# A gated-DeltaNet and latent-attention trunk on one core: the output norm of the first layer moves from POOL to DVE and ACT

## The chip, the core and the metric

The kernel runs on one core of one Trainium2 chip. Its engines work side by side, each through a queue of its own, in order: PE (TensorE, the matmuls, with the weight loads shown as PEld), DVE (VectorE), ACT (ScalarE), POOL (GpSimd) and SP (SyncE, which issues most of the DMAs). The metric is the device time of one execution in microseconds (us), median of three runs.

## The reference

Two layers over 1040 tokens (16 learned ones and 1024 of the sequence), model width 1024, float32. The first layer is a gated DeltaNet with 8 query/key heads and 16 value heads of width 128, the second latent attention with 16 heads. What the change touches is the end of the first layer's mixer: per value head the result `o` is normalised by its root mean square and then multiplied by the gate `z`.

```python
def gdn_mixer(h, w_in, conv_w, a_log, dt_bias, out_norm, w_out):
    proj = h @ w_in
    ...
    o = gated_delta_rule_chunked(q, k, v, beta, g)
    o = rmsnorm(o, out_norm) * jax.nn.silu(z.astype(jnp.float32).reshape(B, L, GDN_V_HEADS, GDN_DV))
    return o.reshape(B, L, GDN_V_W).astype(h.dtype) @ w_out
```

## The kernel before, in words

The first layer fills about the first 1,070 us, the second the rest. Tokens are cut into 9 chunks (16, then eight of 128; `TOK`) and these into three column groups of 400, 384 and 256 (`NCH`). Matrices are split into a high and a low float32r part, and each product is three matmuls (`proj_part`).

The first layer goes through 8 groups `g`, each one query/key head and two value heads. While the recurrence of group `g` runs over its 9 chunks (`rec_chunk`: `ksp`, `r`, `xps`, `x`, `sps`, `S`, `oq`, `o`, one waiting for the other across PE, DVE and ACT), PE is filled with projections of the next groups (`proj_gen`, tiles `pt`). Their weights come by DMA (`raw`), ACT makes the high part (`whi`, L391), POOL the low part (`wlo`, L392), four buffers of each. Beside that DVE builds, for group `g+1`, the inverses of 32-wide triangular blocks (`fill_m`): a chain in which each step needs the one before, alternating products `pr` (L585, L601, L610) with sums (L587 and L613 into `tu`, L603 into `bm`). It starts with L581 and ends with the last L613; ACT copies its pieces (`bm`, L591, L616, L619).

When the last chunk of a column group has its result, `gate(g, ci, ...)` runs: 8 groups times 3 column groups makes 24 calls. POOL makes the mean square with its floor (L813, L814, tile `ov`) and an inverse square root by a start value and three Newton steps of four instructions (`newton_rsqrt`, L138 to L143, tiles `oy` and `ot`): 15 small instructions on 128x8, 128x6 or 128x4 elements. `scale()` then multiplies each chunk's `o` by `oy` (L820, POOL, 128x256, in 72 instructions over all), and after a delay `out_` transposes it on PE (L831, `tp`), multiplies by `z` on DVE (L833, `gt_`) and writes it to `g1scr`. `later(n, fn)` puts work off by n ticks of the fill; so `scale` comes 9 ticks after `gate`, `out_` 14 after `scale`. POOL also makes `kd` (L740) for the recurrence, masks `gcb` (L544) and has the same Newton steps for the keys (`k_stats`, tiles `yk`, `tk`).

Nothing in the text fixes the order on an engine: a scheduler orders the instructions by readiness and priority, so a moved instruction also shifts its neighbours. [...]

Of the kernel before, what the change touches and what calls it, by code (L numbers as in the profile page):

```python
# [15 lines left out]
P = 128  # L16
# [29 lines left out]
def build(nc, tc, A, out, dbg=None):  # L46
# [89 lines left out]
    def newton_rsqrt(e, y, v, t):  # L136

        e.tensor_scalar(y.bitcast(I32), v.bitcast(I32), -0.5, float(0x5F3759DF), op0=ALU.mult, op1=ALU.add)  # L138
        for _ in range(3):
            e.tensor_tensor(t, v, y, op=ALU.mult)  # L140
            e.tensor_tensor(t, t, y, op=ALU.mult)
            e.tensor_scalar(t, t, -0.5, 1.5, op0=ALU.mult, op1=ALU.add)
            e.tensor_tensor(y, y, t, op=ALU.mult)  # L143
# [28 lines left out]
    with contextlib.ExitStack() as g_es:  # L172
# [14 lines left out]
        with tp_(name="xp", bufs=1) as xpool:  # L187
            xts = []
            stats = gp.tile([P, 403], F32, name="stats", tag="xpad", bufs=3)
            xbanks = iter([('tp', 4), ('tp', 4), ('tp', 4), ('tp', 4), ('tp', 4), ('tp', 4), ('tp', 4), ('tp', 4), ('tp', 4), ('tp', 4), ('tp', 4), ('tp', 4), ('tp', 4), ('tp', 4), ('tp', 4), ('tp', 4), ('tp', 4), ('tp', 4), ('tp', 4), ('tp', 4), ('tp', 4), ('tp', 4), ('tp', 4), ('tp', 4)])  # L190
            for (n0, n, cs) in NCH:
                for c in cs:
                    t0, tn = TOK[c]
                    tag = next(xtags)
                    if tag == "MT":
                        xw = gp.tile([P, 8, 2, 128], F32, name="xt", tag=tag, bufs=2).rearrange("p a b c -> p (a b c)")
                        xt = xw[:, :D]
                    elif tag == "mt":
                        xt = xw[:, D:]
                    elif tag:  # L200
                        xt = gp.tile([P, L], F32, name="xt", tag=tag, bufs=2)[:, :D]
                    else:
                        xt = xpool.tile([P, D], F32, name="xt", bufs=5)
                    sp.dma_start(xt[:tn], A["meta_tokens"] if c == 0 else A["x"][t0 - 16:t0 - 16 + tn])
                    if c == 0:
                        junk = gp.tile([P, L], F32, name="junk", tag="vT", bufs=1)[:, :D]
                    ss, rs = stats[:, c:c + 1], stats[:, 16 + c:17 + c]
                    act.activation(junk[:tn], xt[:tn], AF.Square, accum_out=ss[:tn])
                    rstd(gp, rs[:tn], ss[:tn], D, dve if c in (1, 3, 6, 8) else pool)
                    dve.tensor_scalar(xt[:tn], xt[:tn], rs[:tn], None, op0=ALU.mult)  # L210
                    xts.append(xt)

            w_in = A["gdn_w_in"][0].rearrange("(k p) c -> p k c", p=P)
            first_w = []
            first_t = [gp.tile([P, 1024], F32, name="wf", tag=f"u{x}", bufs=1).bitcast(F32R) for x in range(2)]
            for kq in range(4):
                raw = wp.tile([P, 2, 128], F32, name="raw", bufs=4)
                sp.dma_start(raw, w_in[:, 2 * kq:2 * kq + 2, QKW:QKW + 128])
                hl = [first_t[x][:, 256 * kq:256 * kq + 256].rearrange("p (k c) -> p k c", k=2) for x in range(2)]
                act.copy(hl[0], raw)  # L220
                pool.tensor_tensor(hl[1], raw, f(hl[0]), op=ALU.subtract)
                first_w.append(hl)
            first_pts = [ps.tile([P, 512], F32, name="pt", tag="proj", bufs=3) for _ in NCH]
            for pi, (n0, n, cs) in enumerate(NCH):
                for d in range(KT):
                    pt = ps.tile([P, 512], F32, name="pt", **dict(zip(("tag", "bufs"), next(xbanks))))
                    for c in cs:
                        t0, tn = TOK[c]
                        xt = xts[c]
                        pe.transpose(pt[:, t0 - n0:t0 - n0 + tn], xt[:tn, d * 128:(d + 1) * 128], ident[:tn, :tn])  # L230
                    act.activation(hsh[d][:, n0:n0 + n], pt[:, :n], AF.Copy, scale=vecs[:, PN0 + d:PN0 + d + 1])
                    dve.scalar_tensor_tensor(hsl[d][:, n0:n0 + n], pt[:, :n], vecs[:, PN0 + d:PN0 + d + 1],
                                             f(hsh[d][:, n0:n0 + n]), op0=ALU.mult, op1=ALU.subtract)
                for k in range(KT):
                    hi, lo = first_w[k // 2]
                    proj_part(first_pts[pi], hi[:, k % 2], lo[:, k % 2], k, n0, n)
# [568 lines left out]
        def gate(g, ci, os_, oss):  # L805

            s = st[g]
            n0, nn, cs = NCH[ci]
            nc_ = len(cs)
            v = gp.tile([P, 4, 2], F32, name="ov", bufs=2)  # L810
            y = gp.tile([P, 4, 2], F32, name="oy", bufs=3)
            t = gp.tile([P, 4, 2], F32, name="ot", bufs=2)
            pool.tensor_scalar(v[:, :nc_], oss[:, :nc_], 1.0 / 128.0, None, op0=ALU.mult)  # L813
            pool.tensor_tensor(v[:, :nc_], v[:, :nc_], s["q2e"][:, cs[0]:cs[0] + nc_].unsqueeze(2).broadcast_to([P, nc_, 2]), op=ALU.add)  # L814
            newton_rsqrt(pool, y[:, :nc_], v[:, :nc_], t[:, :nc_])

            def scale():
                for i, c in enumerate(cs):
                    n = TOK[c][1]
                    pool.tensor_tensor(os_[i][:n], os_[i][:n], y[:n, i].unsqueeze(2).broadcast_to([n, 2, 128]), op=ALU.mult)  # L820
                later(OUT7 if g == 7 else OUTL, lambda: out_(0), False)

            def out_(h):
                if len(s["z"]) < 2:
                    later(3, lambda: out_(h), False)
                    return
                tp = ps.tile([P, 512], F32, name="tp", tag="tr", bufs=1)

                for i, c in enumerate(cs):
                    t0 = TOK[c][0]  # L830
                    pe.transpose(tp[:, t0 - n0:t0 - n0 + 128], os_[i][:, h], ident)  # L831
                gt_ = gp.tile([P, 400], F32, name="gt_", tag="tanh", bufs=3)
                dve.scalar_tensor_tensor(gt_[:, :nn], tp[:, :nn], onh, s["z"][h][ci], op0=ALU.mult, op1=ALU.mult)  # L833
                r0 = (2 * g + h) % 4 * 128
                (pool if g == 7 else sp).dma_start(g1scr[(2 * g + h) // 4][r0:r0 + 128, n0:n0 + nn], gt_[:, :nn])
                s["gated"] = s.get("gated", 0) + 1
                if h == 0:
                    later(3, lambda: out_(1), False)
            later(SC7 if g == 7 else SCL, scale, False)
# [886 lines left out]
```

## Time and profile before

| | us |
|---|---|
| median of the runs (2162.71, 2164.35, 2171.89) | 2164.35 |
| the profiled execution | 2172.86 |
| its span | 2170.8 |
| PE busy in the span | 2044.1 (94%) |
| DVE, ACT, POOL busy | 1353.9, 1102.1, 745.2 |
| the first layer, about | 1,070 of 2,170.8 |

The profiled execution lies 0.4% above the median. Busy time is that of one engine's instructions; what matters is where PE, the fullest engine, stands idle or runs at the lower of its two clock levels, and which engine it then waits for. A row of the timeline gives the start, the time, the engine, the line, the operation and the tiles; x3 behind it merges three alike in sequence, and in brackets stands the idle time before it and who ended it.

### The profile page before, as it was taken

The page shows a single profiled execution, that of the slowest core. Times are in us where ns is not written, and L with a number is a line of the kernel's source. Part 1 is how long each engine was busy: PE and PEld are TensorE (multiplying, and loading weights), DVE is VectorE, ACT ScalarE, POOL GpSimd, SP SyncE. Part 2 cuts the span into 40 slices and gives each one's busy share as a digit, 9 for nine tenths or more (in the row PEclk, how much of TensorE's full clock was granted, in tenths as well). Part 3 has the DMA queues.
Part 4 walks back from the last instruction along what each step waited for, and adds up shares of the span by engine and source line. Part 5 has one row for each costly group of instructions (what it writes and reads, how often), then busy time and mean ns, then how long its engine had stood idle before and what let it go on. Part 6 is the DMA issues. An engine that isn't in the chain of part 4 may idle for free.

```text
span 2170.8 us, 38605 instructions
## 1 busy us (share of the span) xinstructions
PE 2044.1 (94%) x13407; PEld 1823.2 (84%) x13407; DVE 1353.9 (62%) x3135; ACT 1102.1 (51%) x3323; POOL 745.2 (34%) x1718
## 2 busy tenths in 40 slices
PE   7789889999899999999799999999999999999998
PEld 6789778989899998987576898888999999987886
DVE  6485848585758586765345653436787777885422
ACT  5745545656464746454334453435565656664311
POOL 4442636445554544441301472301304032010111
PEclk9999989999999999999999999999999999999999
DMA  3222122222122222124445431221111111124431
GB/s 119 65 52 60 41 68 58 60 59 64 45 72 54 69 57 63 47 66 110 138 109 171 139 98 61 88 97 45 40 50 40 47 37 50 40 81 163 158 100 41
DMA packets 237419, 164.01 MB, mean 76 GB/s; under 512 B 78476, under 2 KB 217304, under 8 KB 237224
## 3 DMA queue, kind: packets, MB, share of 16 engines
q1 hardware_dynamic: 225472, 140.12, 22.9%
q0 software_dynamic: 4128, 13.15, 1.6%
q10 hardware_dynamic: 7624, 8.27, 1.2%
q8 instruction: 106, 1.74, 0.3%
q14 instruction: 89, 0.73, 0.1%
HBM read 121.27 MB, written 40.19 MB: 74 GB/s over the span
## 4 chain that ended last, share of the span: by engine, by line
PE 57%; DVE 6%; DMA 3%; ACT 2%; POOL 2%; issue 2%; SPq 0%; DVEq 0%; ACTq 0%; POOLq 0%
PE b_a L63 27%; PE b_tr L63 8%; PE pt L63 8%; PE b_pv L63 5%; PE b_tr L1510 3%; PE oq L63 1%; DMA raw<-in_gdn_w_out 1%; DVE pr L585 1%; DMA wraw<-in_gdn_w_out 1%; PE b_tr L1408 1%; PE sps L63 1%; PE b_tr L1504 1%; PE xps L63 1%; PE b_tr L1629 1%; DVE vT L429 1%
## 5 line engine op out<-in xcount | busy, mean ns | idle before, releaser
L63 PE MATMUL pt<-hsh,wlo 128*128 128x400 f32 (+2 forms) x1128 | 370.2, 333 | 17.1 <-POOL wlo L392 17.1
L63 PE MATMUL pt<-hsh,whi 128*128 128x400 f32 (+2 forms) x1128 | 374.4, 333 | 7.4 <-DVE zs L664 3.2
L63 PE MATMUL pt<-hsl,whi 128*128 128x400 f32 (+2 forms) x1128 | 367.5, 326 | 0.0
L392 POOL TENSOR_TENSOR wlo<-raw,whi 128x256 fp32r<-128x256 f32 x188 | 155.6, 833 | 269.5 <-ACT whi L391 251.1
L63 PEld LDWEIGHTS pt<-hsh,wlo 128*128 128x128 f32 x1128 | 213.3, 191 | 20.1 <-POOL wlo L392 19.2
L63 PEld LDWEIGHTS pt<-hsh,whi 128*128 128x128 f32 x1128 | 215.3, 191 | 11.3 <-DVE zs L664 3.6
L63 PEld LDWEIGHTS pt<-hsl,whi 128*128 128x128 f32 x1128 | 214.9, 191 | 1.1
L1486 POOL COPY p<-p 128x32 f32<-128x32 f32 x128 | 28.3, 221 | 338.6 <-ACT p L1483 319.3
L1483 ACT ACTIVATE p<-b_a,mx 128x256 f32<-128x256 f32 (+4 forms) x224 | 120.8, 546 | 39.0 <-DVE mx L1475 17.5
L60 DVE TENSOR_TENSOR ptl<-b_tr,pth 128x512 fp32r<-128x512 f32 x192 | 104.6, 549 | 24.2 <-ACT pth L59 21.9
L59 ACT CAST pth<-b_tr 128x512 fp32r<-128x512 f32 x192 | 91.5, 487 | 52.7 <-PE b_tr L1510 51.3
L1468 DVE TENSOR_REDUCE mx<-b_a 128x1 f32<-128x256 f32 (+4 forms) x224 | 110.9, 504 | 10.5 <-PE b_a L63 7.0
L59 ACT CAST gh<-graw 128x512 fp32r<-128x512 f32 (+1 forms) x86 | 51.1, 602 | 126.2 <-PE b_a L63 87.0
L391 ACT CAST whi<-raw 128x256 fp32r<-128x256 f32 x188 | 75.2, 406 | 66.4 <-PE pt L63 27.5
L60 DVE TENSOR_TENSOR gl<-graw,gh 128x512 fp32r<-128x512 f32 x82 | 55.7, 688 | 82.4 <-ACT gh L59 82.2
L429 DVE SCALAR_TENSOR_TENSOR vT<-xpad,wcv,vT 128x256 f32<-128x256 f32 (+2 forms) x144 | 85.3, 635 | 23.0 <-ACT xpad L423 21.7
L1510 PE MATMUL b_tr<-cm,p 128*128 128x128 f32 x576 | 93.7, 274 | 1.4 <-ACT wt L1390 0.7
L63 PE MATMUL b_a<-hsh,gh 128*128 128x512 f32 (+1 forms) x224 | 88.3, 401 | 6.1 <-ACT ojunk L995 4.2
L1309 DVE SCALAR_TENSOR_TENSOR wlo<-raw,vecs,whi 128x128 fp32r<-128x128 f32 x128 | 44.7, 379 | 72.2 <-ACT whi L1308 69.1
L63 PE MATMUL b_a<-hsl,gh 128*128 128x512 f32 (+1 forms) x224 | 87.9, 400 | 0.3
L740 POOL TENSOR_TENSOR kd<-ktok,kds 128x256 f32<-128x256 f32 x72 | 48.0, 666 | 115.2 <-PE sps L63 114.6
L63 PE MATMUL b_a<-ckth,qah 128*128 128x256 f32 (+4 forms) x224 | 81.5, 364 | 3.2 <-ACT p L1483 3.2
(610 smaller groups left out, 6073.8 us busy)
## 6 DMA issues: line engine op xcount, KB each, us to landing
raw<-in_gdn_w_in SPq DMA_DIRECT2D x192, 128.0 KB
graw<-g1scr SPq DMA_DIRECT2D x52, 256.0 KB
raw<-in_mla_w_in SPq DMA_DIRECT2D x64, 128.0 KB
zscr<-z SPq DMA_DIRECT2D x16, 512.0 KB
zh<-zscr SPq DMA_DIRECT2D x32, 256.0 KB
g2scr<-g2t POOLq DMA_DIRECT2D x32, 256.0 KB, 3.4
graw<-g2scr SPq DMA_DIRECT2D x30, 256.0 KB
wraw<-in_mla_w_out SPq DMA_DIRECT2D x13, 512.0 KB
```

Of the source, the lines that this page charges most:

```text
L59: act.copy(hi, src)
L60: dve.tensor_tensor(lo, src, f(hi), op=ALU.subtract)
L63: pe.matmul(out_, l, r, start=start, stop=stop)
L391: act.copy(hi, raw)
L392: pool.tensor_tensor(lo, raw, f(hi), op=ALU.subtract)
L429: dve.scalar_tensor_tensor(o, xp[:, j:j + n], wc(j), o, op0=ALU.mult, op1=ALU.add)
L740: pool.tensor_tensor(kd, s["ktok"][c].unsqueeze(1).broadcast_to([P, 2, 128]), s["kds"][:, c].unsqueeze(2).broadcast_to([P, 2, 128]), op=AL ...
L1309: dve.scalar_tensor_tensor(lo[:, i], raw[:, i], gk, f(hi[:, i]), op0=ALU.mult, op1=ALU.subtract)
L1468: dve.tensor_reduce(mx[:, i:i + 1], o, axis=AX.X, op=ALU.max, negate=(m == 1))
L1483: act.activation(p[:, bd[i]:bd[i + 1]], pts[i][:, :n], AF.Exp, bias=nm, accum_out=rsum[:, i:i + 1])
L1486: pool.tensor_copy(pm[:, 0:32].rearrange("p (r k) -> p r k", r=2), p[:, 0:16].unsqueeze(1).broadcast_to([P, 2, 16]))
L1510: pe.transpose(tp[:kn, i * 128:(i + 1) * 128], ps4[i][:, 32 + kt0:32 + kt0 + kn], ident)
```

## The change

Three things. In `gate`, the 15 small instructions go from POOL to DVE. In `scale`, each POOL multiply of 128x256 becomes two ACT instructions of 128x128, one per head, which copy with a per-partition factor. And the first `pt` of the transposes is taken before the three first projection tiles, so tag `tp` gets the first four PSUM banks and `proj` the next three.

```diff
--- before.py
+++ after.py
@@ -220,10 +220,12 @@
                 act.copy(hl[0], raw)
                 pool.tensor_tensor(hl[1], raw, f(hl[0]), op=ALU.subtract)
                 first_w.append(hl)
-            first_pts = [ps.tile([P, 512], F32, name="pt", tag="proj", bufs=3) for _ in NCH]
+            first_pts = []
             for pi, (n0, n, cs) in enumerate(NCH):
                 for d in range(KT):
                     pt = ps.tile([P, 512], F32, name="pt", **dict(zip(("tag", "bufs"), next(xbanks))))
+                    if not first_pts:
+                        first_pts = [ps.tile([P, 512], F32, name="pt", tag="proj", bufs=3) for _ in NCH]
                     for c in cs:
                         t0, tn = TOK[c]
                         xt = xts[c]
@@ -810,14 +812,15 @@
             v = gp.tile([P, 4, 2], F32, name="ov", bufs=2)
             y = gp.tile([P, 4, 2], F32, name="oy", bufs=3)
             t = gp.tile([P, 4, 2], F32, name="ot", bufs=2)
-            pool.tensor_scalar(v[:, :nc_], oss[:, :nc_], 1.0 / 128.0, None, op0=ALU.mult)
-            pool.tensor_tensor(v[:, :nc_], v[:, :nc_], s["q2e"][:, cs[0]:cs[0] + nc_].unsqueeze(2).broadcast_to([P, nc_, 2]), op=ALU.add)
-            newton_rsqrt(pool, y[:, :nc_], v[:, :nc_], t[:, :nc_])
+            dve.tensor_scalar(v[:, :nc_], oss[:, :nc_], 1.0 / 128.0, None, op0=ALU.mult)
+            dve.tensor_tensor(v[:, :nc_], v[:, :nc_], s["q2e"][:, cs[0]:cs[0] + nc_].unsqueeze(2).broadcast_to([P, nc_, 2]), op=ALU.add)
+            newton_rsqrt(dve, y[:, :nc_], v[:, :nc_], t[:, :nc_])
 
             def scale():
                 for i, c in enumerate(cs):
                     n = TOK[c][1]
-                    pool.tensor_tensor(os_[i][:n], os_[i][:n], y[:n, i].unsqueeze(2).broadcast_to([n, 2, 128]), op=ALU.mult)
+                    for h in range(2):
+                        act.activation(os_[i][:n, h], os_[i][:n, h], AF.Copy, scale=y[:n, i, h:h + 1])
                 later(OUT7 if g == 7 else OUTL, lambda: out_(0), False)
 
             def out_(h):
```

Lines of the changed kernel are 2 or 3 higher from there on: `wlo` L392 becomes L394, `x` L760 becomes L762, the DVE chain L585, L587, L601, L603 becomes L587, L589, L603, L605. The first 1,217 PE instructions stand as before; in the second layer only a handful of neighbours change places.

POOL in the period of group 4, at the end of the first column group's gate. Before:

```order
L140 TENSOR_TENSOR ot<-ov,oy 128x8
L141 TENSOR_TENSOR ot<-ot,oy 128x8
L142 TENSOR_SCALAR ot<-ot 128x8
L143 TENSOR_TENSOR oy<-oy,ot 128x8
L820 TENSOR_TENSOR o<-o,oy 16x256
L820 TENSOR_TENSOR o<-o,oy 128x256 x3
L392 TENSOR_TENSOR wlo<-raw,whi 128x256 x2
L420 MEMSET xpad 128x3
L392 TENSOR_TENSOR wlo<-raw,whi 128x256
L740 TENSOR_TENSOR kd<-ktok_6497,kds 128x256
```

The same place in the changed kernel:

```order
L394 TENSOR_TENSOR wlo<-raw,whi 128x256
L546 TENSOR_TENSOR gcb<-gcb,cm 128x384 x2
L394 TENSOR_TENSOR wlo<-raw,whi 128x256 x2
L742 TENSOR_TENSOR kd<-ktok_6522,kds 128x256
L394 TENSOR_TENSOR wlo<-raw,whi 128x256 x2
L422 MEMSET xpad 128x3
L394 TENSOR_TENSOR wlo<-raw,whi 128x256
L742 TENSOR_TENSOR kd<-ktok_6522,kds 128x256
```

The Newton steps and the multiplies `o<-o,oy` are gone from ahead of the `wlo` rows.

DVE in the same period, inside the inverse chain. Before:

```order
L601 TENSOR_TENSOR pr<-tu,bm 64x256
L603 TENSOR_REDUCE bm<-pr 64x64
L601 TENSOR_TENSOR pr<-tu,bm 64x512
L603 TENSOR_REDUCE bm<-pr 64x64
L771 SCALAR_TENSOR_TENSOR S<-S,egl,sps 128x128 x2
L601 TENSOR_TENSOR pr<-tu,bm 64x768
L786 TENSOR_TENSOR o<-o,oq 128x256
L603 TENSOR_REDUCE bm<-pr 64x64
L601 TENSOR_TENSOR pr<-tu,bm 64x720
```

After:

```order
L140 TENSOR_TENSOR ot<-ov,oy 128x8
L603 TENSOR_TENSOR pr<-tu,bm 64x256
L141 TENSOR_TENSOR ot<-ot,oy 128x8
L605 TENSOR_REDUCE bm<-pr 64x64
L142 TENSOR_SCALAR ot<-ot 128x8
L603 TENSOR_TENSOR pr<-tu,bm 64x512
L143 TENSOR_TENSOR oy<-oy,ot 128x8
L605 TENSOR_REDUCE bm<-pr 64x64
L140 TENSOR_TENSOR ot<-ov,oy 128x8
L603 TENSOR_TENSOR pr<-tu,bm 64x768
L141 TENSOR_TENSOR ot<-ot,oy 128x8
L773 SCALAR_TENSOR_TENSOR S<-S,egl,sps 128x128 x2
```

The small steps now stand between the products and sums of the chain, mostly one at a time.

ACT in the period of group 3 around `x`, the copy that the recurrence's `sps` waits for. Before:

```order
L391 CAST whi<-raw 128x256
L424 COPY xpad<-pt 128x256
L427 ACTIVATE vT<-pt,wcv 128x256
L760 COPY x<-xps 128x256
L433 ACTIVATE tanh<-vT 128x400
L391 CAST whi<-raw 128x256
```

After:

```order
L393 CAST whi<-raw 128x256
L426 COPY xpad<-pt 128x256
L429 ACTIVATE vT<-pt,wcv 128x256
L823 ACTIVATE o<-o,oy 16x128 x2
L823 ACTIVATE o<-o,oy 128x128 x6
L762 COPY x<-xps 128x256
L435 ACTIVATE tanh<-vT 128x400
L393 CAST whi<-raw 128x256
```

Eight scalings stand directly ahead of `x` and of the next `whi`.

## Rows read from the trace of the kernel before

**Rows 1.** The page: busy us of each engine, its share of the span, instructions.

```profile
PE 2044.1 (94%) x13407; PEld 1823.2 (84%) x13407; DVE 1353.9 (62%) x3135; ACT 1102.1 (51%) x3323; POOL 745.2 (34%) x1718
```

**Rows 2.** Waits of PE from 54 to 1060: for whom, total us, times, longest.

```profile
PE pt L63 <- POOL wlo L392: 17.1, 7, 6.7
...
PE tp L831 <- POOL o L820: 3.8, 4, 2.1
```

**Rows 3.** Timeline of PE, groups 2 to 5: matmuls behind `wlo`, group 4's `xps`, `sps`.

```profile
464.91 0.45 PE L63 MATMUL pt<-hsh,wlo 128*128 128x400 f32 x1 [2.47 <-POOL wlo L392]
...
584.51 0.70 PE L63 MATMUL pt<-hsh,wlo 128*128 128x400 f32 x1 [6.66 <-POOL wlo L392]
...
699.71 0.45 PE L63 MATMUL pt<-hsh,wlo 128*128 128x400 f32 x1 [2.47 <-POOL wlo L392]
...
700.36 0.60 PE L63 MATMUL xps<-r,u 128*128 128x128 f32 x4
...
705.68 0.61 PE L63 MATMUL sps<-x,kd 128*128 128x128 f32 x4
...
814.64 0.45 PE L63 MATMUL pt<-hsh,wlo 128*128 128x400 f32 x1 [2.48 <-POOL wlo L392]
```

**Rows 4.** Timeline of POOL in group 4, just ahead of that matmul.

```profile
694.92 4.06 POOL L820 TENSOR_TENSOR o<-o,oy 16x256 f32<-16x256 f32 x4
698.94 1.41 POOL L392 TENSOR_TENSOR wlo<-raw,whi 128x256 fp32r<-128x256 f32 x2
```

**Rows 5.** Busy time by stretch: three inverse chains, first L581 to last L613.

```profile
core 0: us, PE busy (x) PEld busy (x) DVE busy (x) ACT busy (x) POOL busy (x), PEclk, DMA share, GB/s
223.30:273.80 50.50, 41.87 (x253) 35.96 (x251) 48.71 (x98) 24.80 (x86) 33.48 (x54) 0.93 0.11 35
...
552.20:599.20 47.00, 40.02 (x268) 38.64 (x267) 38.48 (x78) 21.28 (x67) 27.20 (x37) 0.93 0.15 40
671.90:714.20 42.30, 39.52 (x265) 38.00 (x265) 41.14 (x78) 21.18 (x67) 23.25 (x36) 0.96 0.17 45
```

**Rows 6.** The chain that ended last, group 5: start, us, what.

```profile
826.32 0.82 DVE tu L613
...
830.15 0.28 ACT x L760
...
830.57 1.14 PE sps L63 x4
```

**Rows 7.** Timeline of DVE: group 3 (one row), then group 4 beside POOL's gate.

```profile
587.60 0.57 DVE L434 SCALAR_TENSOR_TENSOR vT<-tanh,vT 128x400 f32<-128x400 f32 x1 [6.29 <-ACT tanh L433]
...
683.11 0.77 DVE L585 TENSOR_TENSOR pr<-tu,bm 65x338 f32<-65x338 f32 x1
...
688.21 0.42 DVE L601 TENSOR_TENSOR pr<-tu,bm 64x256 f32<-64x256 f32 x1
688.66 0.41 DVE L603 TENSOR_REDUCE bm<-pr 64x64 f32<-64x256 f32 x1
...
696.22 0.83 DVE L601 TENSOR_TENSOR pr<-tu,bm 64x256 f32<-64x256 f32 x1
...
698.43 0.40 DVE L603 TENSOR_REDUCE bm<-pr 64x16 f32<-64x256 f32 x1
698.76 2.94 DVE L429 SCALAR_TENSOR_TENSOR vT<-xpad,wcv,vT 128x256 f32<-128x256 f32 x3
```

**Rows 8.** Groups by shape: busy us, mean ns of one, idle us before.

```profile
L587 DVE TENSOR_REDUCE tu<-pr 65x4 f32<-65x8 f32 x8 | 1.2, 154 | 0.2
...
L648 ACT ACTIVATE vt<-tp,rki 128x128 f32<-128x128 f32 x144 | 42.5, 372 | 11.8 <-PE tp L645 7.9 <-DVE r L752 3.4 <-POOL ssq L512 0.4
```

**Rows 9.** Timeline of ACT in group 4: four such in sequence.

```profile
732.42 1.13 ACT L648 ACTIVATE vt<-tp,rki 128x128 f32<-128x128 f32 x4
```

**Rows 10.** Busy time by stretch, columns as in rows 5: two stretches at half clock.

```profile
281.10:301.50 20.40, 17.52 (x155) 15.35 (x156) 4.85 (x14) 8.20 (x28) 10.85 (x42) 0.50 0.31 67
...
700.90:704.30 3.40, 3.40 (x15) 3.38 (x14) 3.40 (x6) 0.92 (x3) 0.10 (x1) 0.50 0.25 70
```

## The prediction, made before the changed kernel was run

> **What bounds the kernel now.** I read the page first: PE is busy 94% of the span, 2044.1 of 2170.8 us [rows 1]. So POOL, at 34%, can cost time only where PE waits for it, or where something that PE needs waits for it. The view of waits, cut to the recurrence of the first layer, gives these places: 17.1 us for `wlo`, the largest, and 3.8 us for `o`, both POOL's [rows 2]. Four of the seven waits for `wlo` lie at the same point of groups 2 to 5: 2.47, 6.66, 2.47 and 2.48 us, 14.1 together [rows 3]. POOL's timeline shows what stood ahead: four multiplies `o<-o,oy` in 4.06 us, and only then the two `wlo` [rows 4]. That is the work which the change takes off POOL.
>
> The second question is whether PE could use the time. I read the stretch of each inverse chain on DVE: in group 4 DVE is busy 41.14 of 42.30 us [rows 5], and the chain that ended last runs there in group 5, not through POOL: DVE's last `tu`, then ACT's `x`, then PE's `sps` [rows 6]. So in the periods like this one (chains from 437.2, 671.9, 786.6 and 902.9, all 41 to 43 us) DVE is as late as PE. A PE that no longer waits 2.47 us for `wlo` waits longer at `sps`, unless DVE's chain gets shorter too. In group 3 it is otherwise: the chain takes 47.00 us with DVE busy for 38.48 [rows 5], and DVE itself idles 6.29 us for a `tanh` of ACT [rows 7], which stands behind `x`, which waits for the PE that waits 6.66 us for `wlo`. There POOL is the bound.
>
> **The change, part by part.** *POOL loses* 24 times 15 small steps and 72 multiplies, four of which took 4.06 us [rows 4]. The 14.1 us of waits for `wlo` behind the gate go: in the new order no gate instruction stands ahead of those rows.
>
> *DVE is relieved.* Beside POOL's gate its own instructions last longer. The same product of 64x256 takes 0.42 us at 688.21 and 0.83 at 696.22, next to POOL's steps, and three convolution steps take 2.94 us beside the multiplies [rows 7]. Over the 22 DVE instructions of group 4 that overlap the gate (683.11 the first, 698.76 the last [rows 7]), each against the shortest of its shape, I count 2.8 us. Other POOL work stays, so the relief is between 0 and 2.8 us a chain.
>
> *DVE gains 15 steps a gate.* The nearest row is the sum of 65x8 at 154 ns [rows 8]. If it is placed alone between dependent ones, it may cost nearly nothing: a dependent row starts 0.03 us after the end of the one before (688.21 + 0.42 to 688.66), an independent one 0.07 before it (698.43 + 0.40 to 698.76) [rows 7], so 0.154 - 0.07 - 0.07 fits into the pause. That is the lower end, 0. The upper end is a step that overlaps nothing: 0.154 + 0.03 = 0.19, times 15 = 2.8 us, just the relief. In the chains the steps stand mostly one at a time between dependent rows, so I take 0.05 each, nearest to the lower end: 0.8 us. Net -2.0 us for each of the four chains: **-8.0**. For the chain of group 0, from 223.3 with DVE busy 48.71 of 50.50 [rows 5], with two gates' steps in it, I take the same **-2.0** (0 to -4); for that of group 1, whose gate touches only its end, **-1.0**. Group 3 falls from 47.0 to the 42.3 of its like: **-4.7** (0 to -6.7).
>
> [...]
>
> *ACT gains* 144 copies of 128x128. The nearest row is `vt`, 372 ns alone [rows 8], four in sequence 1.13 us [rows 9], so about 0.28 each: 2.3, 1.7 and 1.1 us for blocks of 8, 6 and 4. Eight blocks of each make 41 us, on an engine busy for 51% [rows 1] and 21 of 42 us in the chains [rows 5]. Queued behind a block are `x`, for which PE's `sps` waits, `whi`, for which POOL and then PE wait, and `tanh`. What hides it: projection matmuls stand on PE between `xps` and `sps`, from 700.36 to 705.68 in group 4 [rows 3], so `x` has time. Were that cover gone, the price is the whole 41 us. I charge 0.15 us a block: **+3.6** (0 to 41).
>
> *Transposes of `o`* wait 3.8 us for POOL today, nearly all in the last group, where no fill is left [rows 2]. DVE and ACT do the steps in less, but in order behind weight splits that wait for DMAs; of the 3.8 I take **-1.5** (+3 to -3.8).
>
> *Clock.* [...] The short stretches lie under DVE's chain, 0; of the long one, behind the chain of group 0, I take a quarter: **-2.0** (0 to -8.8).
>
> *PSUM banks.* No instruction changes by this alone; the second layer keeps its order but for a few neighbours: 0, within half a us either way. Its cover is that no bank is shared more than before; if it were, one transpose's wait would show.
>
> Sum: -8.0 - 2.0 - 1.0 - 4.7 + 3.6 - 1.5 - 2.0 = **-15.6 us**. The profiled execution took 2172.86 us, its span 2170.8; 2172.9 - 15.6 = 2157.3, a ratio of 0.9928. On the median of 2164.35 that is 2148.8, rounded 2149 us.
>
> **The rivals.** *First, the steps eat the relief.* If each small step costs its full 0.19 us, the four chains and those of groups 0 and 1 gain nothing (+8.0 + 2.0 + 1.0), PE's wait for `wlo` reappears at `sps`, and -4.6 is left: about 2160. For it speaks that DVE is already full in these chains [rows 5]; against it the overlapped starts [rows 7]. [...]
>
> *Second, slower: the scalings stand in front of the recurrence.* ACT works in order, and a block waits for the last Newton step, which in DVE's order stands behind convolution and chain rows. If `xps` is done by then, `x` is late by the block, on average 1.7 us (41 / 24), and `sps`, `S`, `ksp` and `r` of the chunk after it. At full price, 41 instead of 3.6, the sum is -15.6 - 3.6 + 41 = +21.8, or 2186. It decides from 0.8 us a block on, where 24 blocks equal the 19.2 us of gain. For it: in groups 1, 3 and 5 the eight stand directly ahead of `x`. Against it: ACT is half idle in the chains [rows 5], and 5.3 us lie between `xps` and `sps` [rows 3]. [...]
>
> *Third, more comes back.* If the waits for `wlo` go in full (14.1), those for `o` too (3.8), the long half-clock stretch vanishes (8.8), the chain of group 0 gives 4, and four short stretches like that of group 4 give half of 3.40 us each (6.8), the sum is -37.5: 2135.4 for this execution, 2127 on the median.
>
> *That the change does not do what it says* is excluded for the instructions, since the new order shows them on DVE and ACT.
>
> **How the numbers follow.** My forecast, a gain of 11 to 30 us, gets 0.55; the third rival 0.08; the first, and any mix in which gain and ACT's price meet within 0.5%, 0.25; the second 0.12. A measurement of this kernel can tell about 0.5%, 11 us, from no change: faster 0.63, same 0.25, slower 0.12. The range from 2127 to 2168 reaches to the third rival below and past the first above (2160, with the tail's +3 and some of ACT's price), and leaves out half of the second and what lies beyond the others.
>
> **What would show it.** Right: no wait of PE for `wlo` behind the gate in groups 2 to 5; the chains of 42 us at about 40 and that of group 3 near them; DVE's products beside the gate at their short times; the small steps near 0.15 us. Wrong: chains of 42 us or more, waits for `wlo` turned into waits for `x` at `sps`, more PE waits for ACT, a longer stretch from 1030 to 1075 in the last group. What would make it wrong most easily is a new order in which ACT's blocks hold `x` or `whi` in every group, or half-clock stretches that I counted as hidden.

## The result and the profile after

The changed kernel takes 2182.17 us at the median (2174.57 to 2188.65), the kernel before beside it 2165.01 (2161.18 to 2171.89): a ratio of 1.0077, 95% interval 1.0063 to 1.0092. It is slower by 17 us, above the range of the prediction and on the other side of no change. The profiled execution took 2181.69 us with a span of 2179.9, against the 2170.8 of before, whose profiled execution lay 8 us over its own median; the two traces side by side thus show some 9 of the 17 us.

The engines' busy time, from the page after, beside [rows 1]: POOL fell by 159 us, DVE rose by 58.5, ACT by 39, and PE did the same work.

```profile
PE 2044.7 (94%) x13407; PEld 1821.8 (84%) x13407; DVE 1412.4 (65%) x3495; ACT 1140.9 (52%) x3467; POOL 586.5 (27%) x1286
```

The waits of PE from 54 to 1060 (for whom, total us, times, longest), beside [rows 2]:

```profile
PE xps L63 <- DVE r L754: 20.5, 17, 2.7
PE pt L63 <- ACT xpad L425: 15.6, 15, 1.8
...
PE pt L63 <- POOL wlo L394: 1.6, 1, 1.6
...
PE tp L834 <- ACT o L823: 1.2, 1, 1.2
```

The waits for `wlo` fell from 17.1 us to 1.6, as predicted. In their place stand waits for `xpad`: ACT's copies that empty a projection tile and so set its PSUM bank free for the next `pt`. In each of groups 2 to 5 they stand at the first product of that series of `pt` whose fifth product waited for `wlo` in [rows 3]. From PE's timeline (start, time, instruction, in brackets the idle time before it):

```profile
464.44 0.70 PE L63 MATMUL pt<-hsh,whi 128*128 128x400 f32 x1 [1.48 <-ACT xpad L425]
...
580.52 0.45 PE L63 MATMUL pt<-hsh,whi 128*128 128x400 f32 x1 [1.29 <-ACT xpad L425]
...
705.01 0.45 PE L63 MATMUL pt<-hsh,whi 128*128 128x400 f32 x1 [1.48 <-ACT xpad L425]
...
821.64 0.45 PE L63 MATMUL pt<-hsh,whi 128*128 128x400 f32 x1 [0.83 <-ACT xpad L425]
```

In the kernel before, that first product found its bank just free. In group 4, from ACT's timeline and from PE's, the last copy of `xpad` ended at 694.37 and the product began at 694.41:

```profile
694.21 0.16 ACT L423 COPY xpad<-pt 128x3 f32<-128x3 f32 x1
...
694.41 0.45 PE L63 MATMUL pt<-hsh,whi 128*128 128x400 f32 x1
```

PE's wait for DVE's `r` at `xps`, 12.0 us before, has become the largest, 20.5.

Why `xpad` is late in group 4 is read on ACT's timeline. `jk` (the square of `o`) waits 3.80 us for DVE's `o`, which stands among the chain and the new steps, and `xpad` stands behind `jk`. Later the scalings wait 1.11 us for the last step, and `whi`, the chain's `bm` and `tanh` stand behind them:

```profile
703.19 0.31 ACT L802 ACTIVATE jk<-o 128x128 f32<-128x128 f32 x1 [3.80 <-DVE o L788]
...
703.94 0.47 ACT L426 COPY xpad<-pt 128x400 f32<-128x400 f32 x1
...
711.04 2.46 ACT L823 ACTIVATE o<-o,oy 16x128 f32<-16x128 f32 x8 [1.11 <-DVE oy L143]
713.41 0.39 ACT L393 CAST whi<-raw 128x256 fp32r<-128x256 f32 x1
713.70 0.27 ACT L618 COPY bm<-tu 65x48 f32<-65x48 f32 x1
...
714.19 0.83 ACT L435 ACTIVATE tanh<-vT 128x384 f32<-128x384 f32 x2
```

In groups 2, 3 and 5 as well `xpad` stands behind a `jk` that waited, by 2.61 to 3.80 us. ACT's waits from 360 to 965 for DVE's `o` (total us, times, longest), first before, then in the changed kernel:

```profile
ACT jk L800 <- DVE o L786: 24.1, 20, 2.8
...
ACT jk L802 <- DVE o L788: 38.1, 18, 3.8
```

Three inverse chains (groups 2, 3, 4), busy time by stretch, the columns as in [rows 5]:

```profile
439.70:482.30 42.60, 38.67 (x249) 36.97 (x248) 41.47 (x94) 22.33 (x70) 14.47 (x16) 0.92 0.16 41
556.70:599.80 43.10, 38.55 (x266) 36.55 (x264) 42.37 (x94) 23.57 (x75) 15.46 (x18) 1.00 0.17 44
680.20:723.00 42.80, 36.51 (x251) 34.63 (x249) 42.00 (x94) 22.17 (x70) 15.36 (x16) 1.00 0.15 41
```

POOL is relieved (15.36 us busy against 23.25), but DVE is as full as before (42.00 of 42.80) and the chain no shorter than the 42.30 of before. Of the chains of groups 2 to 6 only group 3's came down by more than 0.6 us, from 47.00 to 43.10. From one chain's end to the next, groups 2 to 6 took 121.2, 117.5, 123.1, 117.2 and 116.2 us, where before they took 115.7, 119.8, 115.0, 115.3 and 114.8.

### The profile page after: what moved, and what is told of

It reads as the page before. It is cut to its first block, busy times and chain, and to the rows that moved or that the text cites. A ratio compares the mean times of both kernels' runs of the same rounds, so it can differ in the third digit from the quotient of the medians.

```text
span 2179.9 us, 38735 instructions
## 1 busy us (share of the span) xinstructions
PE 2044.7 (94%) x13407; PEld 1821.8 (84%) x13407; DVE 1412.4 (65%) x3495; ACT 1140.9 (52%) x3467; POOL 586.5 (27%) x1286
## 4 chain that ended last, share of the span: by engine, by line
PE 64%; DVE 18%; DMA 7%; ACT 5%; issue 3%; POOL 2%; SPq 1%; DVEq 0%; ACTq 0%; POOLq 0%
PE b_a L63 27%; PE pt L63 12%; PE b_tr L63 8%; PE b_pv L63 5%; PE b_tr L1513 3%; DVE pr L587 3%; DVE tu L589 2%; PE oq L63 1%; DVE vT L431 1%; DVE pr L612 1%; DMA bm<-mscr 1%; DMA mscr<-MT 1%; DVE pr L603 1%; PE sps L63 1%; DVE bm L605 1%
## 5 line engine op out<-in xcount | busy, mean ns | idle before, releaser
L63 PE MATMUL pt<-hsh,whi 128*128 128x400 f32 (+2 forms) x1128 | 376.6, 335 | 22.4 <-ACT xpad L425 15.6
L63 PE MATMUL pt<-hsl,whi 128*128 128x400 f32 (+2 forms) x1128 | 371.9, 330 | 0.0
L394 POOL TENSOR_TENSOR wlo<-raw,whi 128x256 fp32r<-128x256 f32 x188 | 164.9, 883 | 367.9 <-ACT whi L393 348.1
L1486 ACT ACTIVATE p<-b_a,mx 128x256 f32<-128x256 f32 (+4 forms) x224 | 120.8, 546 | 38.8 <-DVE mx L1478 17.1
L59 ACT CAST gh<-graw 128x512 fp32r<-128x512 f32 (+1 forms) x86 | 51.2, 602 | 127.2 <-PE b_a L63 87.7
L431 DVE SCALAR_TENSOR_TENSOR vT<-xpad,wcv,vT 128x256 f32<-128x256 f32 (+2 forms) x144 | 80.5, 598 | 21.7 <-ACT xpad L425 20.5
```

Of the source, the lines that this page charges most:

```text
L59: act.copy(hi, src)
L63: pe.matmul(out_, l, r, start=start, stop=stop)
L394: pool.tensor_tensor(lo, raw, f(hi), op=ALU.subtract)
L431: dve.scalar_tensor_tensor(o, xp[:, j:j + n], wc(j), o, op0=ALU.mult, op1=ALU.add)
L1486: act.activation(p[:, bd[i]:bd[i + 1]], pts[i][:, :n], AF.Exp, bias=nm, accum_out=rsum[:, i:i + 1])
```

## The experiments

The theories: A, the steps on DVE are the loss; B, ACT's scalings are; C, the order of the PSUM banks is. All times are medians beside runs of the kernel before on the same chip.

| kernel | us | before | ratio (95% interval) |
|---|---|---|---|
| e1: steps on DVE alone | 2177.95 | 2163.99 | 1.0063 (1.0048 to 1.0078) |
| e2: scalings on ACT alone | 2177.84 | 2163.99 | 1.0064 (1.0050 to 1.0078) |
| e3: PSUM banks alone | 2163.40 | 2163.99 | 0.9998 (0.9986 to 1.0009) |
| e4: steps and scalings, old banks | 2178.45 | 2163.99 | 1.0074 (1.0058 to 1.0091) |
| e5: neither steps nor scaling | 2141.15 | 2163.42 | 0.9888 (0.9865 to 0.9911) |
| e6: scalings on ACT, no steps | 2139.65 | 2163.42 | 0.9886 (0.9863 to 0.9908) |
| e7: steps on DVE, no scaling | 2153.44 | 2163.42 | 0.9955 (0.9930 to 0.9980) |
| e8: steps on POOL, no scaling | 2146.83 | 2163.42 | 0.9916 (0.9898 to 0.9934) |
| e9: changed, scalings a chunk later | 2166.27 | 2164.92 | 1.0007 (0.9994 to 1.0021) |
| e10: steps on POOL, scalings on ACT, later | 2161.30 | 2164.92 | 0.9990 (0.9976 to 1.0004) |
| e11: changed, 11 steps in place of 15 | 2170.55 | 2164.92 | 1.0032 (1.0016 to 1.0047) |
| e12: before, multiplies later | 2153.44 | 2164.92 | 0.9949 (0.9932 to 0.9966) |
| e13: e6 with the scalings later | 2161.72 | 2165.30 | 0.9983 (0.9967 to 0.9999) |
| e14: e10 with 13 ticks for 18 | 2170.06 | 2165.30 | 1.0017 (0.9998 to 1.0035) |
| e15: e12 with 13 ticks for 18 | 2163.38 | 2165.30 | 1.0001 (0.9986 to 1.0017) |
| e16: e9 with 11 steps | 2166.90 | 2165.30 | 1.0008 (0.9994 to 1.0022) |
| e17: e10, last group not later | 2159.64 | 2165.14 | 0.9980 (0.9966 to 0.9993) |
| e18: e12 with 22 ticks | 2161.73 | 2165.14 | 0.9997 (0.9981 to 1.0013) |

### One part alone

**e1**, only the steps on DVE:

```diff
-            newton_rsqrt(pool, y[:, :nc_], v[:, :nc_], t[:, :nc_])
+            newton_rsqrt(dve, y[:, :nc_], v[:, :nc_], t[:, :nc_])
```

(and the two instructions for `v` ahead of it).

> One part alone: the 15 steps of the norm on DVE, the multiplies stay on POOL, PSUM banks as before. Before 2165, changed 2182. Theory A (the loss comes from the steps on DVE: in the trace of the changed kernel the 15 rows of a gate take 4.2 to 4.7 us of DVE's time in a chain, not the 2.3 that 0.15 each would make, and o, jk and the evictions xpad stand behind them): slower, 2172 to 2185. Theory B (the loss comes from ACT's scalings, which stand ahead of xpad, tanh and x): not slower, 2155 to 2167. Theory C (the loss comes from the other order of the PSUM banks): as before, 2165 +-4, or a gain.

**e2**, only the scaling on ACT:

```diff
-                    pool.tensor_tensor(os_[i][:n], os_[i][:n], y[:n, i].unsqueeze(2)...
+                    for h in range(2):
+                        act.activation(os_[i][:n, h], os_[i][:n, h], AF.Copy, scale=y[:n, i, h:h + 1])
```

> One part alone: the 72 multiplies as 144 scalings on ACT, the steps stay on POOL, banks as before. Theory A: same or faster, 2150 to 2166, with no waits of PE for wlo behind the gate. Theory B: slower, 2172 to 2185, with PE waiting for xpad or x as in the changed kernel. Theory C: as before or a gain.

**e3**, only the first `pt` of the transposes taken ahead of the three projection tiles.

> One part alone: only the order in which the PSUM banks are handed out. Theories A and B: 2165 +-3 (within 0.2% of before). Theory C: slower, 2172 to 2185.

**e4**, everything but that:

```diff
-            first_pts = []
+            first_pts = [ps.tile([P, 512], F32, name="pt", tag="proj", bufs=3) for _ in NCH]
...
-                    if not first_pts:
-                        first_pts = [ps.tile([P, 512], F32, name="pt", tag="proj", bufs=3) for _ in NCH]
```

> The changed kernel with the order of the PSUM banks of before, that is steps on DVE and scalings on ACT only. Theories A and B: 2182 +-4, as the changed kernel. Theory C: 2150 to 2167.

Theory C falls: the order of the banks makes no difference that can be measured (0.6 us of 2164). A and B each stood against the other, and both were half right: either part alone costs 14 us, both together no more (14.5 with the old banks). In e1 the chain is longer. This is its stretch for group 4, against 42.30 in [rows 5]:

```profile
677.50:722.00 44.50, 39.44 (x268) 37.48 (x267) 43.77 (x93) 21.30 (x67) 21.37 (x22) 0.98 0.16 42
```

In e2 the chain is longer too, by less outside group 4 (44.3 in group 4, 43.0 to 43.3 in groups 2, 3 and 5, where e1 has 44.4 to 44.8), and ACT stands still. Its timeline in group 4:

```profile
695.96 0.40 ACT L821 ACTIVATE o<-o,oy 16x128 f32<-16x128 f32 x1 [4.56 <-POOL oy L143]
...
696.55 2.14 ACT L821 ACTIVATE o<-o,oy 16x128 f32<-16x128 f32 x7
698.60 0.39 ACT L391 CAST whi<-raw 128x256 fp32r<-128x256 f32 x1
698.89 0.30 ACT L800 ACTIVATE jk<-o 128x128 f32<-128x128 f32 x1
...
699.20 0.47 ACT L424 COPY xpad<-pt 128x400 f32<-128x400 f32 x1
```

And PE's matmul, the first product of the series that had the old wait:

```profile
700.24 0.70 PE L63 MATMUL pt<-hsh,whi 128*128 128x400 f32 x1 [2.96 <-ACT xpad L423]
```

The scalings wait 4.56 us for POOL's last step, and the `xpad` that empties PE's bank stands behind them. `wlo` was late by 2.47 us before; `xpad` is late by 2.96 now.

The two parts lose at different waits of PE. The sums from 54 to 1090 of e1:

```profile
PE xps L63 <- DVE r L752: 24.9, 16, 4.6
...
PE pt L63 <- ACT xpad L423: 6.6, 7, 1.3
```

and of e2:

```profile
PE pt L63 <- ACT xpad L423: 15.1, 11, 3.0
PE xps L63 <- DVE r L752: 10.9, 14, 2.2
```

The changed kernel has both, 20.5 and 15.6 us. Why 14 us and 14 us make only 14.5 no run here shows.

The profile of e3 shows one thing more. Its instructions are those of before, but its chain of group 3 took 42.40 us where [rows 5] has 47.00:

```profile
543.90:586.30 42.40, 39.62 (x266) 38.12 (x265) 41.29 (x78) 21.08 (x67) 23.21 (x36) 0.96 0.17 45
```

and PE's wait there was 2.47 us where [rows 3] has 6.66:

```profile
571.76 0.59 PE L63 MATMUL pt<-hsh,wlo 128*128 128x400 f32 x1 [2.47 <-POOL wlo L394]
```

So the long chain of group 3 was, as far as these two profiles tell, an accident of one execution. It is not the only such place. The two profiled spans differ by 15.8 us (2170.8 and 2155.0; the medians by 0.6). Taken from one chain's end to the next, 4.2 of it lie in group 3 and 5.5 in group 1, where the long half-clock stretch of [rows 10] stands (e3 has two of 6.8 us there); 4.9 lie behind the last chain (130.1 and 125.2 us).

### Steps and scaling apart

Four kernels leave out parts of the norm, so that what is left can be priced by itself. **e5** has neither steps nor scaling, **e7** and **e8** make the factors and don't use them, **e6** scales by the sum of squares:

```diff
+                        act.activation(os_[i][:n, h], os_[i][:n, h], AF.Copy, scale=oss[:n, i, h:h + 1])
```

> The kernel before with the steps and the scaling of the output norm left out (the results stay unnormalised; the sums of squares stay). It tells what the gate costs on POOL in all, the most that a move could gain. Theory A2 (the wait for wlo and the contention are real costs, and the two new places each cost about as much): 2140 to 2152, 12 to 24 us under before. Theory B2 (the chain of DVE bounds the groups whatever POOL does, so nothing was to be gained): 2158 to 2166.

> Steps left out, scalings on ACT with the sum of squares as factor in place of the norm's: the 144 scalings without any wait for the steps. Against the kernel without the norm: Theory A2 (ACT's price is the wait for the factor, 24 to 38 us of idle ACT in front of the scalings, with xpad and x behind it; the 28 us of scalings themselves are hidden): +0 to +4 us. Theory B3 (it is the time of the scalings itself): +8 to +15 us.

> Steps on DVE, scaling left out (the factors are made and not used). Against the kernel without the norm: Theory A2 (the steps cost DVE's time in the chains, 0.28 us each by the mean of 225 rows in the changed kernel, 4.2 us a gate, over 8 chains of which 7 have a gate's steps): +14 to +26 us. Theory B2 (they fit into pauses of the chain and only what waits for the factor costs): +0 to +6 us.

> Steps on POOL, scaling left out (the factors are made and not used). Against the kernel without the norm: Theory A2 (POOL's multiplies are what makes wlo late, the small steps cost little): +0 to +5 us, so the multiplies are worth 8 us or more. Rival: the steps, which stand between the wlo and disturb DVE, cost as much as the multiplies: +6 to +12 us.

The differences to before in us, by where the steps (rows) and the scaling (columns) are:

| | no scaling | POOL | ACT |
|---|---|---|---|
| no steps | -22 | not run | -24 |
| steps on POOL | -17 | 0 | +14 |
| steps on DVE | -10 | +14 | +14 (old banks), +17 (changed) |

There was something to gain: the gate cost 22 us on POOL, 6 for the steps and 16 for the multiplies. The steps on DVE cost 12 us, a little under what A2 wanted for e7 (14 to 26) and twice the most that B2 allowed. Those on POOL cost 5.7, between the two ranges of e8. The scalings on ACT cost nothing where no step stands ahead of them, and 24 to 31 us where they wait for steps. In e6 they stand right behind `jk` and are ready. For 360 to 965, the group of e6 (count, busy us and mean ns of one, then the idle time in front and who ended it):

```profile
L818 ACT ACTIVATE o<-o,oss 128x128 f32<-128x128 f32 (+1 forms) x100 | 36.1, 400 | 0.0
```

and that of the changed kernel:

```profile
L823 ACT ACTIVATE o<-o,oy 128x128 f32<-128x128 f32 (+1 forms) x90 | 28.0, 389 | 24.2 <-DVE oy L143 24.2
```

The relief of DVE and the price of the steps are both visible in the chain of group 4, first of e5:

```profile
653.30:693.70 40.40, 38.60 (x270) 37.23 (x268) 39.30 (x78) 21.43 (x67) 17.68 (x18) 1.00 0.17 47
```

then of e7:

```profile
659.40:702.10 42.70, 38.67 (x268) 36.96 (x266) 41.95 (x94) 21.30 (x67) 18.04 (x18) 1.00 0.16 44
```

Without the gate on POOL the chain is 1.9 us shorter than the 42.30 of [rows 5]; with the steps on DVE it is 2.3 us longer again. The relief lies in the convolution and the products, here for the chain of group 4, of the kernel before:

```profile
L585 DVE TENSOR_TENSOR pr<-tu,bm 65x8 f32<-65x8 f32 (+13 forms) x14 | 8.1, 577 | 0.3
L429 DVE SCALAR_TENSOR_TENSOR vT<-xpad,wcv,vT 128x400 f32<-128x400 f32 (+2 forms) x9 | 6.7, 775 | 0.0
```

and of e5:

```profile
L585 DVE TENSOR_TENSOR pr<-tu,bm 65x8 f32<-65x8 f32 (+13 forms) x14 | 7.4, 526 | 0.3
L429 DVE SCALAR_TENSOR_TENSOR vT<-xpad,wcv,vT 128x400 f32<-128x400 f32 (+2 forms) x9 | 5.6, 656 | 0.0
```

### The place of the scalings, and fewer steps

The scheduler puts the scalings where it takes the factor to be ready. To move them, **e9**, **e10** and **e12** let the factor go through one more small DVE instruction that also reads the newest state, times zero (e9, lines cut short):

```diff
-        OUTL, SCL = 14, 9
+        OUTL, SCL = 5, 18
...
             def scale():
+                yl = gp.tile([P, 4, 2], F32, name="oyl", bufs=2)
+                dve.scalar_tensor_tensor(yl..., hold["lastS"][:, 0, :2 * nc_], 0.0, y..., op0=ALU.mult, op1=ALU.add)
```

**e11** keeps the place and makes a Newton step of three instructions in place of four, and `v` of one in place of two.

> The changed kernel, but the factors for ACT go through one more small DVE instruction that also reads the newest state S (times zero), and scale comes 18 ticks after the gate in place of 9 (out_ 5 after it in place of 14): in ACT's order the scalings stand about one chunk later, when the steps are done. Theory W (the loss of the changed kernel is ACT's wait for the factors, 24 us from 360 to 965, with xpad, jk and x in the queue behind it; the scalings themselves are free): 2152 to 2162, with ACT's wait in front of the scalings under 5 us. Theory M (the scalings cost by their time wherever they stand, once the real order is kept): 2172 to 2184.

> Steps on POOL as before, scalings on ACT, put about one chunk later in the same way. Theory W: the price of the steps on POOL without the multiplies (2147) and little more: 2146 to 2156, faster than both kernels. Theory M: 2172 to 2182, as with the scalings on ACT at their old place (2178).

> The changed kernel with 11 steps on DVE in place of 15 (two operations in one instruction where DVE has them; same three Newton steps). Theory W with the steps' own price (12 us for 15 steps, by the kernels without the scaling): 4/15 of 12 is 3 us, and the factor comes earlier by 4 places in the queue, a quarter of the 27 us of waiting: 2168 to 2176. If only the steps' own time counts: 2175 to 2179. If neither: 2180 +-3.

> The kernel before (steps and multiplies on POOL) with the multiplies put about one chunk later in the same way. It splits the 16 us by which the multiplies on POOL cost more than steps alone. If it is POOL's wait for the factor and the place of the multiplies ahead of wlo: 2150 to 2158. If it is the multiplies' time and their contention with DVE wherever they stand: 2160 to 2167.

In e9 the wait in front of the scalings fell from 24.2 us to 6.3, that of `jk` for DVE's `o` from 38.1 to 24.6, and with them the time from 2182 to 2166. So the wait was a large part of the loss. But 11 us over e7 stay, each taken beside its own runs of before, and e9 lies over what theory W wanted (2162 at most, under 5 us of wait), though under M's range. e10 came to 2161, where W wanted at most 2156. e11 took some 10 us off and met its first case (2168 to 2176); its wait in front of the scalings is 18.8 us. e12 met its first case, and is the fastest kernel here that does the whole work: 2153.44, 0.9949.

**e13** puts the scalings later without any steps. **e14** and **e15** change the delay only, and **e16** joins e9 and e11.

> Steps left out, scalings on ACT a chunk later, by the same DVE instruction with the newest S (factor: the sum of squares). Beside 2140 for the scalings at their old place without steps. If the later place itself costs the 13 to 14 us that are left with the steps: 2151 to 2156. If what is left is the coupling to the steps (still some waits, and POOL's or DVE's steps in the way): 2138 to 2144.

> Steps on POOL, scalings on ACT, delayed by 13 ticks in place of 18, out_ 10 ticks after. In ACT's order the scalings stand between jk and the convolution's evictions. If the wait for the factor alone decides: between 2161 (18 ticks) and 2178 (no delay), 2163 to 2172. If the lateness was the price: under 2160.

> Steps and multiplies on POOL, the multiplies delayed by 13 ticks in place of 18, out_ 10 ticks after. Between 2153 (18 ticks) and 2164 (no delay): 2150 to 2162. At or under 2153, the delay isn't needed in full.

> 11 steps on DVE in place of 15, and the scalings on ACT a chunk later (18 ticks). With 15 steps it was 2166. If the steps' own price adds up (4/15 of 12): 2161 to 2165. If fewer steps also take the rest of the waiting: 2152 to 2160. If the gain of fewer steps was only the shorter wait, which the later place has taken already: 2164 to 2168.

e13 came out slower than both its cases: scalings that come late cost some 20 us over e6 (22 by the medians, 20 beside each one's runs of before), with only 3.5 us of waits in front of them. That is more than e9 and e10 had left over (11 and 13), so these parts don't add up either, and what the 24 added DVE instructions cost by themselves no run shows. Between the two profiled spans (2135.5 and 2161.9), 10 of the 26 us lie behind the last chain, from its end to the first matmul of the second layer, where the profiles of before and e3 differ by 4.9. In e6:

```profile
917.80:1038.90 121.10, 109.53 (x778) 89.49 (x776) 60.49 (x159) 67.69 (x227) 14.19 (x23) 0.97 0.40 113
```

In e13:

```profile
932.00:1063.20 131.20, 114.74 (x777) 92.74 (x777) 62.45 (x163) 70.25 (x231) 14.09 (x23) 0.94 0.38 107
```

Another 9 lie in groups 2 to 6, between 0.4 and 2.9 us in each. e14 landed between its neighbours, as a shorter delay should. e15 missed its range (2150 to 2162) by 1.4 us. e16 gained nothing over e9, so with the wait gone fewer steps save nothing that can be measured.

Two attempts at a better version: **e17** is e10 with the last group's scalings not held back, **e18** is e12 with a longer delay.

> Steps on POOL, scalings on ACT a chunk later in groups 0 to 6 only; in the last group they don't wait for a later state. With all groups late it was 2161, and 128.3 us from the last chain's end to the first matmul of the second layer. If the end of the layer pays for lateness: 2151 to 2157, that stretch at 118 to 123 us. If not: 2159 to 2164.

> Steps and multiplies on POOL, the multiplies delayed by 22 ticks in place of 18 (out_ 3 ticks after in place of 5). No delay gave 2164, 13 ticks 2163, 18 ticks 2153. If the gain comes from being behind wlo and grows no further: 2150 to 2157. If lateness has its price here too: 2158 to 2168.

Neither met its first case; both fell into the second. In e17 the stretch behind the last chain took 127.2 us, not 118 to 123, so the last group's own lateness was not what it pays for; e17 still beats the kernel before by 0.2%. e18 lost e12's gain. With 13, 18 and 22 ticks the multiplies on POOL give 2163, 2153 and 2162: no trend. What e12 gains by is not settled. Its wait for `wlo` is down to 10.0 us from 17.1, but in e15 and e18 it is 5.4 and 4.1, without the gain. Some ten microseconds of such a difference may be how the order happened to fall, and the same holds for single comparisons of that size above.

## Why the prediction was wrong

**The waits for `wlo`**: right that they go, wrong that PE would have their 14.1 us. The prediction asked what is late next and looked at `sps` and `x`, but the waits for `x` at `sps` fell from 7.6 us to 5.0. Late next were `r` at `xps` (12.0 to 20.5 us) and `xpad` (1.7 to 15.6): the first product of the same series needs the bank that `xpad` frees, and before, in group 4, it had been free only 0.04 us ahead. The prediction had looked at the queue of ACT for `x`, `whi` and `tanh` and left out the evictions, which stand in the same queue and which PE needs for the same series of matmuls.

**ACT's scalings**: the step that failed. It put 0.15 us a block, +3.6, by the scalings' own time and the cover that 5.3 us between `xps` and `sps` give. The runs show that the own time is hidden (e6 against e5: -1.5 us) and that the price is the wait for the factor, 24 to 31 us: 24.2 us of idle ACT in 14 places, 1.7 each, with everything behind it held. In group 4 the path to PE is not a direct one, since `xpad` stands there ahead of the scalings, behind `jk`. What ties the price to the scalings is that e9, which only moved them, brought both of ACT's waits down and took 16 of the 27 us with them; the other 11 stay open.

The second rival named this wait, said that a block waits for the last step in DVE's order, and gave its threshold, 0.8 us a block. That its 2186 came near to 2182 is luck: it priced the blocks by their own time, 41 us, and looked for the loss at `sps`, where the wait for `x` fell. Its chance of 0.12 rested on ACT being half idle and on the cover for `x`; ACT, busy for 52% of the span, was no cover for the 24.2 us of wait in its queue. It named groups 1, 3 and 5 as the bad ones, where the eight stand directly ahead of `x`; measured, the longest groups were 2 and 4 (121.2 and 123.1 us, in e4 121.0 and 121.4), where `x` goes first and `whi`, `bm` and `tanh` stand behind.

By e6 (-1.5 us against e5) the multiplication as such was no loss on ACT here; the loss was where it had to wait.

**DVE's relief**: right, and in its upper half: 1.9 us of the chain of group 4 between before and e5, where 0 to 2.8 was given and 2.8 was used.

**DVE's steps**: the term was mis-sized. It took 0.05 us each, 0.8 a chain; e7 against e5 shows 2.3 in the chain of group 4 and 12 us over all. In the changed kernel's first layer the 360 steps took 249 ns in the mean. Sorted by whether POOL computed meanwhile, 248 ran alone, mean 161 ns, none over 200; 112 ran beside a POOL instruction, mean 445 ns, 68 of them over 200 with a mean of 630. All 68 began after a POOL instruction and ended 15 to 74 ns after its end. The 44 others began before the POOL instruction (20), within 15 ns of its start (7) or in its last 215 ns (17). Four rows of DVE in group 4:

```profile
693.76 0.99 DVE L815 TENSOR_SCALAR ov<-oss 128x8 f32<-128x8 f32 x1
...
698.51 0.69 DVE L143 TENSOR_TENSOR oy<-oy,ot 128x8 f32<-128x8 f32 x1
...
699.73 0.15 DVE L140 TENSOR_TENSOR ot<-ov,oy 128x8 f32<-128x8 f32 x1
...
707.30 0.66 DVE L142 TENSOR_SCALAR ot<-ot 128x8 f32<-128x8 f32 x1
```

and four of POOL at the same times (the two `gcb` end at 694.73, the first and the last `wlo` at 699.19 and 707.94; the step at 699.73 began 0.01 us after its `wlo` and paid nothing):

```profile
691.72 3.01 POOL L546 TENSOR_TENSOR gcb<-gcb,cm 128x384 f32<-128x384 f32 x2 [4.72 <-DMA gcb<-gcscr]
...
698.07 1.12 POOL L394 TENSOR_TENSOR wlo<-raw,whi 128x256 fp32r<-128x256 f32 x1 [2.65 <-ACT whi L393]
...
699.72 0.77 POOL L394 TENSOR_TENSOR wlo<-raw,whi 128x256 fp32r<-128x256 f32 x1
...
706.31 1.63 POOL L394 TENSOR_TENSOR wlo<-raw,whi 128x256 fp32r<-128x256 f32 x1 [5.82 <-ACT whi L393]
```

The prediction had read this contention for the long rows (0.42 against 0.83 us, [rows 7]) and took the short ones at the price of a row alone, though `wlo`, `gcb` and `kd` stay on POOL. The trace of the changed kernel looks like a block rather than a shared speed, since all 68 hindered steps end within 15 to 74 ns after the POOL instruction, though a step alone takes 161 ns; what holds them no run shows. So the first rival was right on the chains: they stayed at 42 to 43 us, not 40, at 0.15 us a step (2.3 / 15) where it had 0.19 and the sum 0.05.

**Group 3**: the chain fell to 43.1 as said, but the -4.7 was no gain: e3 shows 42.4 with the old work. A term was built on one execution's odd row.

**Transposes of `o`**: their wait for `o` fell from 3.8 to 1.2 us (the one for ACT's `vt` rose from 1.7 to 6.8, which the prediction had not asked for), and the stretch from the last chain's end to the second layer from 130.1 to 127.8, about the -1.5 that stood in the sum. But e3 shows 125.2 there with the old work, so the runs don't show that the term came true.

**Clock**: the long stretch at 0.50 behind group 0 is gone: two of 3.4 and 6.8 us stand there now, in place of the 20.4 of [rows 10]. That is no gain of the change either: e3, with the old work, has two of 6.8 there, and e4, with the new work, one of 13.7 and two shorter ones. And the waits at the ends of later chains are followed by longer stretches and new ones, so from 360 to 965 the granted clock was 0.50 for 40.8 us, where it had been so for 30.6. Two in the changed kernel, behind the waits that end groups 3 and 4:

```profile
599.90:606.70 6.80, 5.67 (x21) 4.70 (x22) 2.71 (x7) 4.43 (x17) 1.78 (x4) 0.50 0.52 142
...
722.80:729.60 6.80, 5.38 (x20) 4.38 (x20) 1.90 (x6) 4.32 (x15) 2.37 (x4) 0.50 0.43 120
```

No run shows the 8.8 us that work at 0.50 was to lose, of which -2.0 is about a quarter and which the third rival counts in full, nor the half of each short stretch there; what the runs showed is that group 1 took 5.5 us less in e3, with two stretches of 6.8 us in place of the 20.4. So two terms, -4.7 and -2.0, were built on odd places of one execution.

**PSUM banks**: 0, within half a microsecond, was right as far as can be measured (0.6 us, within the interval of e3).

Put together by the runs, on top of the kernel without the norm (2141): the steps on DVE +12, the scalings that wait for them +27 (2180 between e4 and the changed kernel), against the +22 that the gate cost on POOL; 17 more is what was measured (the +27 is the rest of this sum, not a run of its own). In the prediction's terms: of the 33 us between -15.6 and +17, some 23 are ACT's scalings, +27 in place of +3.6, and some 9 the rest, -10 by e7 in place of -19.2, most of it DVE's steps. What stays open: why scalings that come late with little waiting cost some 20 us (e13), beyond where the time appears; why the costs of e1 and e2 don't add up; and why e12's delay of 18 ticks gains what 13 and 22 don't.

## What to carry to other kernels

When work moves to an engine with an ordered queue, price the wait for its input first and its own time second (here 24.2 us of idle ACT, against scalings that cost nothing when ready), and list everything that stands behind it in that queue, down to the copies that only set a buffer free. When a wait is taken from one place, ask what the instructions around it need next; here the bank of the same series had come free only 0.04 us ahead of its use. Before a term is built on a row that stands out from its like in other groups, count it as an accident, or take a second profile of the same kernel.

## What the runs showed of the hardware

In the changed kernel a small DVE instruction of 128x4 to 128x8 took 161 ns alone (mean of 248 rows, none over 200). Of the 112 that ran beside a POOL instruction, 68 took over 200 ns, 630 in the mean; all of these began after its start and ended 15 to 74 ns after its end. The 44 others came before the POOL instruction or within some 15 ns of its start (27 rows), or in its last 215 ns (17). Two parts that each cost 14 us (e1 and e2) cost 14.5 together (e4), though alone they lose at different waits of PE: 24.9 us for `r` in e1, 15.1 for `xpad` in e2. And 100 scalings on ACT with a mean of 0.40 us cost nothing while ready (e6 against e5: -1.5 us), though they keep the engine busy for 36.1 us.
